# Splitting mixed tiles into f16 parts first and turning them by transposing DMAs

## The chip, the cores and the metric

The kernel runs on one core of a Trainium2 chip. The metric is the device time of one execution in microseconds, the median of the runs; a profiled execution gives the trace. Engines: PE multiplies matrices (PEld loads its weights), DVE, ACT and POOL work elementwise, SP issues most DMAs.

## The reference

One layer of a bidirectional encoder over 4096 tokens and 16 prepended meta tokens, width 1024. Two head groups stand side by side; their outputs are joined, gated and projected:

```python
u = rmsnorm(h, norm_g[i])
proj = jnp.einsum('bld,de->ble', u, w_in[i])
f_in, f_gate, q, k, v, a_gate = jnp.split(proj, SPLIT_POINTS, axis=-1)
f_out = fourier_branch(f_in, w_fmix[i], b_fmix[i]) * jax.nn.silu(f_gate)
a_out = attention_branch(q, k, v, q_norm_g[i], k_norm_g[i], cos, sin, n_tok) * jax.nn.silu(a_gate)
mixed = jnp.concatenate([f_out, a_out], axis=-1)
h = h + jnp.einsum('ble,ed->bld', mixed, w_out[i])
```

`fourier_branch` is the real part of a 2-D DFT over positions and 64 channels in 8 groups, then a linear map per group. `attention_branch` has 8 query heads and 2 key/value heads of 64, over all 4112 tokens. A final RMSNorm follows.

## The kernel before

Products of f32 precision are made from f16 parts: a number x is kept as its f16 rounding and the f16 remainder ("hi" and "lo"), and three f16 matmuls (hi by hi, hi by lo, lo by hi) stand for one f32 matmul.

`phase_a` projects all tokens and prepares the Fourier inputs. `phase_b`, which the change touches, has these stages.

- An early loop. The Fourier half is made in units (`seq`: 8 even, one odd remainder, 8 odd, one last): `dft_units` multiplies by DFT matrices into `pd`, `gather` copies `pd` to the f32 tile `stk` on ACT (L870 to L873), `trans` turns `stk` on PE (L895) and splits it to `thl` on ACT, DVE and POOL (L897 to L902), and `mix` applies the linear map on PE (L86 to L88), adds the bias and multiplies by the gate `fgu`. In this loop `mix` evicts PSUM with two ACT instructions (L949) and POOL adds the bias (L954) and multiplies (L956). The result `mo`, f32, is stored to `mf_d` in DRAM by the next `release`. Seven units pass here, while PE also computes row maxima of scores (L1040, reduced on DVE at L1041).
- 32 pairs: 8 blocks of 512 queries by 4 head pairs. `stream` gives a pair 66 steps (two heads by 33 key tiles). Step j makes a score tile on PE (`qk`, L1108 and L1109, into one of two PSUM buffers `s`), its exponential on ACT (L1112), and the f16 remainder on POOL or DVE (L1114). The weighted sum with the values (`pvm`, L1129 to L1136) runs LAG = 5 steps behind. Pairs 0 to 3 also carry the other ten Fourier `mix` units, through `block0`; there DVE evicts and adds the bias (L951) and POOL multiplies (L956).
- In pairs 4 to 31 the output projection of the block before goes along, 128 tokens for each pair. At step TR = 12 `out_tr` takes the f32 Fourier tile `mf` (128x512, loaded from `mf_d`) and the f32 attention tile `obs` (128x512), turns both by eight PE transposes into a PSUM tile of the `m` buffers (L1172), makes the hi part on ACT (L1175), and one step later the lo part on DVE (`low`, L1177). `out_units` then makes 24 matmuls for each of two column halves, one for each step from O0 = 15 and O1 = 39 on (L1189); its index j counts three matmuls for each of eight row blocks, four of `mf` first, then four of `obs`.
- A tail for the last block: `tail_tr(s, part)` transposes `mf` or `obs` of row tile s (L1354) and splits it into `hv` and `lv`, which lie in the buffers of `qA` and `qB`; `tail_mm` and `tail_end` project and normalise.

The order of instructions on each engine is the order in which the code emits them; an engine does not pass a waiting instruction. The DMAs named here go through SP's queue in program order.

## Time and profile before

| | |
|---|---|
| median of three runs | 3243.61 us (3240.65 to 3244.94) |
| span of the profiled execution | 3240.9 us |
| TensorE clock granted, mean | 0.997 |
| from the transposes of pair 4 to those of pair 31 (L1172 starts at 1140.1 and ends its starts at 3128.9) | 27 pairs, 73.7 us each |

The profiled execution's own time is not listed apart from the three runs; its span lies 2.7 us under their median. In rows of instructions the first two numbers are start and length in us, then engine, line, operation, output tile<-inputs and shape; what stands in square brackets is the time that the engine was idle before, and what ended it. In groups, "x28: a/b/c" gives count and least, median and greatest length in ns.

### The profile page before, as it was taken

Reading aid. Unit: us, or ns where it says so; the run is one execution under the profiler, and the core shown is the slowest. Engines: PE = TensorE matmul, PEld = TensorE weight load, DVE = VectorE, ACT = ScalarE, POOL = GpSimd, SP = SyncE. Lnnn points to the kernel's source line nnn. Section 1 sums busy time; section 2 is a strip of 40 time slices with the busy share of each in tenths; the row PEclk is TensorE's granted clock in tenths of the full one; section 3 lists DMA queues with packets and bytes.
Section 4 is the critical chain, followed back from the end, with each engine's and each line's share of the span. In section 5 each row is a group of like instructions: output and inputs, shape, how many; then the busy total and the mean of one; then the engine's idle time right before and its main releaser. Section 6 shows DMA issues by size and latency. Waiting matters only on the chain.

```text
span 3240.9 us, 78233 instructions
## 1 busy us (share of the span) xinstructions
PE 3189.1 (98%) x32919; PEld 1879.4 (58%) x32919; DVE 2375.5 (73%) x3246; ACT 1703.2 (53%) x2969; POOL 2264.4 (70%) x2172
## 2 busy tenths in 40 slices
PE   8999999998999999999999999999999999999998
PEld 4665555555666655555555555555555555555564
DVE  7656566647677777777777778777777877778764
ACT  5443433434555555555555555555555555555553
POOL 4655455536777778777777777777787777777762
PEclk9999999999999999999999999999999999999999
DMA  7443344638322210002001000100110020000011
GB/s 249 134 160 138 136 154 145 198 140 250 118 78 85 77 50 21 21 21 63 21 21 47 21 21 24 47 21 21 33 52 21 21 47 21 25 21 21 21 37 59
DMA packets 139572, 232.00 MB, mean 72 GB/s; under 512 B 22131, under 2 KB 78275, under 8 KB 136275
## 3 DMA queue, kind: packets, MB, share of 16 engines
q1 hardware_dynamic: 125394, 201.83, 19.8%
q10 hardware_dynamic: 13824, 25.17, 2.1%
q8 instruction: 257, 4.21, 0.5%
q14 instruction: 97, 0.79, 0.1%
HBM read 160.58 MB, written 66.38 MB: 70 GB/s over the span
## 4 chain that ended last, share of the span: by engine, by line
PE 91%; DVE 4%; issue 2%; DMA 1%; ACT 1%; POOL 1%; SPq 0%; ACTq 0%; POOLq 0%; DVEq 0%
PE s L1109 14%; PE s L1108 14%; PE o L1129 13%; PE po L1189 9%; PE m L1040 8%; PE o L1136 8%; PE ps L303 5%; PE ps L304 5%; PE ps L306 4%; PE o L1134 2%; PE o L1132 2%; PE pd L857 2%; PE m L1369 1%; PE m L1172 1%; PE pf L86 1%
## 5 line engine op out<-in xcount | busy, mean ns | idle before, releaser
L1114 POOL TENSOR_TENSOR rr<-pe 128x512 f16<-128x512 f32 x1572 | 1680.3, 1085 | 523.4 <-ACT pe L1112 517.9
L1112 ACT ACTIVATE pe<-s 128x512 f32<-128x512 f32 x2112 | 1260.3, 597 | 1031.8 <-PE s L1109 880.6
L1041 DVE TENSOR_REDUCE mx<-m 128x2 f32<-128x1024 f32 x1024 | 1205.7, 1219 | 174.7 <-PE m L1040 169.3
L1136 PE MATMUL o<-VV,rr 128*128 128x65 f16 x8448 | 975.9, 193 | 0.0
L1136 PEld LDWEIGHTS <-rr 128*128 128x128 f16 x8448 | 785.5, 98 | 168.8 <-POOL rr L1114 1.5
L1129 PE MATMUL o<-VV,pe 128*128 128x129 f16 x6336 | 841.0, 222 | 0.5 <-ACT tt L1140 0.4
L1109 PE MATMUL s<-qB,K 128*128 128x512 f16 x2112 | 800.6, 379 | 1.4 <-DVE qB L1076 1.4
L1129 PEld LDWEIGHTS <-pe 128*128 128x128 bf16 x6336 | 591.2, 98 | 362.1 <-issue 191.3
L1108 PE MATMUL s<-qA,K 128*128 128x512 f16 x2112 | 799.8, 379 | 0.7 <-ACT pe L1112 0.7
L1114 DVE TENSOR_TENSOR rr<-pe 128x512 f16<-128x512 f32 x540 | 450.5, 835 | 230.3 <-ACT pe L1112 225.9
L1132 PE MATMUL o<-VV,pe 128*128 128x65 f16 x2112 | 411.5, 195 | 0.0
L1134 PE MATMUL o<-VV,pe 128*128 128x64 f16 x2112 | 410.7, 194 | 0.0
L303 PE MATMUL ps<-wh,xh 128*128 128x512 f16 (+2 forms) x1032 | 353.3, 354 | 8.0 <-ACT xh L291 8.0
L304 PE MATMUL ps<-wl,xh 128*128 128x512 f16 (+2 forms) x1032 | 353.1, 354 | 2.7 <-DVE wl L274 2.7
L1040 PE MATMUL m<-K,qP 64*128 64x512 f16 x2048 | 313.2, 382 | 6.5 <-DMA qP<-q_d 2.4
L306 PE MATMUL ps<-wh,xl 128*128 128x512 f16 x768 | 292.1, 380 | 0.0
L1134 PEld LDWEIGHTS <-pe 128*128 128x128 bf16 x2112 | 209.2, 99 | 0.0
L1132 PEld LDWEIGHTS <-pe 128*128 128x128 bf16 x2112 | 206.6, 98 | 0.0
L1109 PEld LDWEIGHTS <-K 128*128 128x128 f16 x2112 | 205.2, 97 | 1.7 <-issue 1.6
L1108 PEld LDWEIGHTS <-K 128*128 128x128 f16 x2112 | 203.5, 96 | 0.9 <-issue 0.4
L1040 PEld LDWEIGHTS <-qP 64*128 64x128 f16 x2048 | 59.9, 94 | 226.5 <-issue 224.0
L1189 PE MATMUL po<-woh,mh 128*128 128x512 f16 x448 | 169.8, 379 | 0.9 <-DVE hh L1194 0.9
(213 smaller groups left out, 3561.1 us busy)
## 6 DMA issues: line engine op xcount, KB each, us to landing
room<-x SPq DMA_DIRECT2D x32, 512.0 KB
xt<-xt SPq DMA_DIRECT2D x32, 512.0 KB
sg<-fx SPq DMA_DIRECT2D x16, 1024.0 KB
xr<-x SPq DMA_DIRECT2D x32, 512.0 KB
out<-yo SPq DMA_DIRECT2D x32, 512.0 KB
ct<-cdo SPq DMA_DIRECT2D x9, 1088.0 KB
fg_d<-g ACTq DMA_DIRECT2D x32, 256.0 KB
ag_d<-g ACTq DMA_DIRECT2D x32, 256.0 KB
```

What stands on the lines that cost most here:

```text
L303: T.matmul(o, xh[:, d, :n], wh[:, d, c0:c1], start=d == 0, stop=False)
L304: T.matmul(o, xh[:, d, :n], wl[:, d, c0:c1], start=False, stop=False)
L1040: T.matmul(t[:, e], q[rs, s, p], K[kv][rs, 4 * c:4 * c + 4, 0], start=True, stop=True)
L1041: V.tensor_reduce(mx[:, s, :, c], t, axis=AX.X, op=ALU.max)
L1108: T.matmul(s, K[kv][:, t, 0], qa, start=True, stop=False)
L1109: T.matmul(s, K[kv][:, t, 1], qb, start=False, stop=True)
L1112: S.activation(pe, s, AF.Exp, scale=HD ** -0.5)
L1114: eng.tensor_tensor(out=rr, in0=pe, in1=hi, op=ALU.subtract)
L1129: T.matmul(o[:, c0:c0 + 129], hi[:, cs], va, start=t == 0 and s == 0, stop=t == NT, skip_group_check=True)
L1132: T.matmul(o[:, c0:c0 + 65], hi[:, cs], vh, start=False, stop=t == NT, skip_group_check=True)
L1134: T.matmul(o[:, c0:c0 + 64], hi[:, cs], vl, start=False, stop=t == NT, skip_group_check=True)
L1136: T.matmul(o[:, c0:c0 + 65], rr[:, cs], vh, start=False, stop=t == NT, skip_group_check=True)
```

## The change

The mixed tiles are split into hi and lo parts before they are turned, and the turning is done by DMAs that transpose 2-byte data.

- Fourier half: `mix` itself makes the two f16 parts, hi on ACT and lo on POOL, for both halves (`ver`) of a unit, and `mf_d` holds 1024 f16 numbers for a token in place of 512 f32 (the same bytes). The parts lie in `hlx` or in the buffers of `mt` and `at`.
- Attention half: `out_tr` makes hi from `obs` on ACT, `low` makes lo on DVE and issues the transposing DMA into `at`.
- `load_mf` is now a transposing DMA from `mf_d` into `mt`, issued at step 53 of the pair ahead.
- The matmuls read `mt` and `at`; the 224 PE transposes of pairs 4 to 31 are gone.
- Tail: eight transposing DMAs at step 20 of the last pair bring the Fourier halves into `hv` and `lv`; `tail_tr` turns the attention half alone, with 16 PE transposes in place of 32.

```diff
+        bs = w2.tile([P, 2, 512], F32, tag="xr", name="bs")
+        bias, stk8 = bs[:, 0], bs[:, 1]
+        hlx = w2.tile([P, 2, 2, 512], F16, tag="xr", name="hlx")
+        hls = [[hlx[:, i] for i in range(2)],
+               [w1.tile([P, 2, 512], F16, tag=n, name="hl" + n) for n in ("mt", "at")]]
...
             G.tensor_tensor(out=mo[:n], in0=mo[:n], in1=fgs.pop(u)[:n], op=ALU.mult)
+            hl = hls[u % 2]
             for ver in range(2):
+                S.activation(hl[ver][:n, 0], mo[:n, ver], AF.Copy)
+                G.tensor_tensor(out=hl[ver][:n, 1], in0=mo[:n, ver], in1=hl[ver][:n, 0], op=ALU.subtract)
                 for p0, m, t0, st in runs_of(u, ver):
-                    held.append((rows(mf_d, t0, m, st), mo[p0:p0 + m, ver]))
+                    held.append((rows(mf_d, t0, m, st), hl[ver][p0:p0 + m].rearrange("p w c->p (w c)")))
...
         def load_mf(b, s):
-            mf = w2.tile([P, 512], F32, tag="mf", name="mf")
-            dma(mf, mf_d[b * QB + s * P:b * QB + s * P + P])
-            pst[b, s] = [mf, None]
+            mt = w1.tile([P, 8, P], F16, tag="mt", name="mt")
+            dma_t(mt, mf_d[b * QB + s * P:b * QB + s * P + P])
+            mts[b, s] = [mt]
...
         def out_tr(b, s):
-            mf, xr = pst[b, s]
-            t = pm.tile([P, 2, 512], F32, tag="m", name="m")
-            tv = t.rearrange("p a (b c)->p (a b) c", c=P)
-            for j in range(8):
-                src = mf[:, j * P:(j + 1) * P] if j < 4 else obs[b][:, s, (j - 4) * P:(j - 3) * P]
-                T.transpose(tv[:, j], src, id32)
-            mh = ld["sh1"].tile([P, 8, P], F16, tag="mh", name="mh")
-            ml = ld["sh1"].tile([P, 8, P], F16, tag="ml", name="ml")
-            S.activation(mh, tv, AF.Copy)
-            pst[b, s] = [mh, ml, xr]
-            return lambda: V.tensor_tensor(out=ml, in0=tv, in1=mh, op=ALU.subtract)
+            src = obs[b][:, s]
+            hl = ld["sh1"].tile([P, 2, 512], F16, tag="ml" if s % 2 else "mh", name="ah")
+            S.activation(hl[:, 0], src, AF.Copy)
+
+            def low():
+                V.tensor_tensor(out=hl[:, 1], in0=src, in1=hl[:, 0], op=ALU.subtract)
+                at = w1.tile([P, 8, P], F16, tag="at", name="at")
+                dma_t(at, hl.rearrange("p w c->p (w c)"))
+                mts[b, s].append(at)
+
+            return low
...
-                T.matmul(d["po"], (ml if w == 2 else mh)[:, i],
+                T.matmul(d["po"], mts[b, s][i // 4][:, i % 4 + (4 if w == 2 else 0)],
...
             if i > 4:
-                out_load(b - 1, p)
+                load_xr(b - 1, p)
...
+                if i >= 4 and j == 53 and i + 1 < len(pairs):
+                    load_mf(*divmod(i - 3, 4))
...
                 if j == 20 and i + 1 == len(pairs):
-                    load_mf(b, 0)
-                    load_mf(b, 1)
+                    for x in range(4):
+                        t0 = b * QB + x * P
+                        dma_t(hv[:, 8 * x:8 * x + 4], mf_d[t0:t0 + P, 0:512])
+                        dma_t(lv[:, 8 * x:8 * x + 4], mf_d[t0:t0 + P, 512:1024])
                     load_xr(b, 0)
...
-        def tail_tr(s, part):
-            src = pst[b, s][0] if part == 0 else obs[b][:, s]
+        def tail_tr(s):
+            src = obs[b][:, s]
```

The changed code is longer, so line numbers move: L949 is L953 in the changed kernel, L956 L960, L1112 L1119; the copies in `mix` are L963, its subtractions L964, `load_mf` L1162, `low`'s DMA L1177.

Three places in the order of instructions. The first is ACT in the early loop, from one unit's eviction to the next, before and now (`mo` the mixed unit, `stk` the gathered next one, `thl` its split):

```order
L949 ACTIVATE mo<-s 128x512 x2
L870 ACTIVATE stk<-pd 128x4x64
L872 ACTIVATE stk<-pd 128x4x2
L873 ACTIVATE stk<-pd 128x4x2x31
L897 ACTIVATE thl<-s 128x512
L898 ACTIVATE thl<-thl 128x512
L949 ACTIVATE mo<-s 128x512 x2
```

```order
L953 ACTIVATE mo<-s 128x512 x2
L963 ACTIVATE hlx<-mo 128x512 x2
L874 ACTIVATE stk<-pd 128x4x64
L876 ACTIVATE stk<-pd 128x4x2
L877 ACTIVATE stk<-pd 128x4x2x31
L901 ACTIVATE thl<-s 128x512
L902 ACTIVATE thl<-thl 128x512
L953 ACTIVATE mo<-s 128x512 x2
```

Two copies, which read `mo` after POOL's multiplication, now stand ahead of the next unit's gather. The second place is ACT in pairs 0 and 1, around the first odd unit (`pe` the exponentials, `tt` a head's eviction):

```order
L897 ACTIVATE thl<-m 128x512
L898 ACTIVATE thl<-thl 128x512
L1112 ACTIVATE pe<-s 128x512 x13
L1140 ACTIVATE tt<-o 128x452
L1112 ACTIVATE pe<-s 128x512 x5
```

```order
L901 ACTIVATE thl<-m 128x512
L902 ACTIVATE thl<-thl 128x512
L1119 ACTIVATE pe<-s 128x512 x11
L963 ACTIVATE hlmt<-mo 128x512
L963 ACTIVATE hlat<-mo 128x512
L1119 ACTIVATE pe<-s 128x512 x2
L1147 ACTIVATE tt<-o 128x452
L1119 ACTIVATE pe<-s 128x512 x5
```

The two copies of the unit stand between two exponentials. The third place is SP in two consecutive pairs of the steady part:

```order
L1222 DMA out<-yo 128x1024
L1155 DMA mf<-mf_d 128x512
L1160 DMA xr<-x 128x1024
L811 DMA ag<-ag_d 128x4x128
L1222 DMA out<-yo 128x1024
```

```order
L1224 DMA out<-yo 128x1024
L1162 DMA_TRANSPOSE mt<-mf_d 128x8x128
L1167 DMA xr<-x 128x1024
L811 DMA ag<-ag_d 128x4x128
L1177 DMA_TRANSPOSE at<-ah 128x8x128
L1224 DMA out<-yo 128x1024
```

The load of the Fourier half is a transposing DMA, and a second one, for the attention half, stands between the gate load and the store of the output.

## Prediction

> **What bounds the kernel now.** I read the page's busy times and the chain that ended last first, then the sums over four stretches of the span, and only then single instructions where the diff puts new ones. On the page:

> ```profile
> span 3240.9 us, 78233 instructions
> PE 3189.1 (98%) x32919; PEld 1879.4 (58%) x32919; DVE 2375.5 (73%) x3246; ACT 1703.2 (53%) x2969; POOL 2264.4 (70%) x2172
> PE 91%; DVE 4%; issue 2%; DMA 1%; ACT 1%; POOL 1%; SPq 0%; ACTq 0%; POOLq 0%; DVEq 0%
> ```

> PE carries nine tenths of the chain, so PE time taken away should come off the end, and PE time lost to a new wait should be added to it. By stretch (start:end, length, busy time of PE, PEld, DVE, ACT, POOL, granted clock, DMA):

> ```profile
> 720.00:797.00 77.00, 63.40 (x577) 41.94 (x575) 54.93 (x66) 29.87 (x63) 48.20 (x30) 1.00 0.72 224
> 797.00:1116.00 319.00, 313.80 (x3809) 206.72 (x3808) 229.69 (x238) 170.56 (x312) 245.82 (x240) 1.00 0.33 101
> 1140.00:3100.00 1960.00, 1959.84 (x22709) 1132.43 (x22708) 1549.68 (x1787) 1116.01 (x1887) 1524.53 (x1544) 1.00 0.10 30
> ```

> The first is the early Fourier loop (PE 82%), the second the attention pairs 0 to 3 with Fourier units mixed in (98%), the third attention with the output projection (100%). The removed transposes lie in the third and in the tail; the new splits of the Fourier half lie in the first two, which the words of the change do not tell.

> **Steady part: transposes removed.** PE in the last pair, at the step with the transposes, and one ACT group:

> ```profile
> 3128.53 0.60 PE L1172 MATMUL m<-id,mf 128*128 128x128 f32 x4
> 3128.97 0.60 PE L1172 MATMUL m<-id,ob 128*128 128x128 f32 x4
> 3129.40 0.22 PE L1129 MATMUL o<-VV,pe 128*128 128x129 f16 x1
> L1175 ACT ACTIVATE mh<-m x28: 1023/1023/1024, 1141.2 to 3129.6; 128x1024 f16<-128x1024 f32 x28
> ```

> Eight transposes take 3129.40 - 3128.53 = 0.87 us of PE's queue, 28 times: -24.4 us. Since PE has no idle time there, all of it should come off. The split that stays becomes half as long on ACT and DVE and reads SBUF; both have slack (57% and 79% of the third stretch), so I cost it at nothing.

> What must now be in time is the transposing DMA into `at`: issued at step 13, first read at step 27. The thirteenth projection matmul of the last pair, and the one long DMA that the chain shows:

> ```profile
> 3143.82 0.38 PE L1189 MATMUL po<-woh,mh 128*128 128x512 f16 x1
> 820.42 12.79 DMA acs<-acs_d
> ```

> That step is the tightest: no maximum units lie between. Without the transposes the matmul comes at 3142.95; I put the f16 parts ready near 3130.4 (step 13 at 3128.9, and 1.5 us for copy and subtraction), which leaves 12.5 us. `acs<-acs_d` moves 2 MB in 12.79 us, so 256 KB at that rate are 1.6 us; the upper bound I take is that whole 12.79, which would just cost nothing or a few tenths. So: cost 0, ends 0 and some 10 us. `mt` is issued at step 53 and read at step 15 of the next pair, twice as long. On SP's queue `at` stands behind the gate load, the queue's longest waiter:

> ```profile
> SPq L811 <- POOL ob L1146: 1157.0, 30, 68.4
> ```

> It waits for POOL's output rows of the previous pair's second head, which by the lag of five steps come at step 4 or 5, so the queue is free before step 13; behind `at` stands only the output store. The eight DMAs of the last pair have from step 20 to the pair's end, over 40 us.

> **Tail.**

> ```profile
> 3203.10 0.60 PE L1354 MATMUL s<-id,mf 128*128 128x128 f32 x4
> 3210.03 0.66 PE L1354 MATMUL s<-id,mf 128*128 128x128 f32 x4 [0.71 <-DVE qB L1358]
> ```

> Sixteen transposes go (16 x 0.109 = 1.7 us), and the 0.71 us wait for a PSUM buffer that the `mf` transposes of row tile 2 filled: -2.5 us.

> **Early loop: the new wait.** mix() now puts two ACT copies behind ACT's two evictions. They read what POOL's multiplication writes, and ACT's next work (gather and split of the following unit) stands behind them. One unit before, from add to add on POOL, with the ACT, PE and DVE rows of the next unit:

> ```profile
> 746.43 2.34 POOL L954 TENSOR_TENSOR mo<-mo,bias 128x1024 f32<-128x1024 f32 x1 [4.67 <-DMA bias<-bias]
> 782.74 2.36 POOL L954 TENSOR_TENSOR mo<-mo,bias 128x1024 f32<-128x1024 f32 x1 [1.50 <-ACT mo L949]
> 785.18 2.35 POOL L956 TENSOR_TENSOR mo<-mo,fgu 128x1024 f32<-128x1024 f32 x1
> 789.59 2.35 POOL L954 TENSOR_TENSOR mo<-mo,bias 128x1024 f32<-128x1024 f32 x1 [1.50 <-ACT mo L949]
> 783.35 0.38 ACT L870 ACTIVATE stk<-pd 128x256 f32<-128x256 f32 x1 [0.68 <-PE pd L854]
> 783.68 0.39 ACT L873 ACTIVATE stk<-pd 128x248 f32<-128x248 f32 x1
> 784.12 0.66 PE L895 MATMUL s<-id,stk 128*128 128x128 f32 x4
> 786.51 0.68 DVE L901 TENSOR_TENSOR thl<-s,thl 128x512 f16<-128x512 f32 x1
> L378 ACT ACTIVATE qs<-t 128x512 f16<-128x512 f32 x32 | 19.9, 623 | 46.4 <-POOL t L363 46.4
> L1114 POOL TENSOR_TENSOR rr<-pe 128x512 f16<-128x512 f32 x1572 | 1680.3, 1085 | 523.4 <-ACT pe L1112 517.9
> ```

> Before, ACT gathers the next unit while POOL works, and the cycle is POOL's add, multiplication, copy and 1.50 us of waiting: 6.85 us. After, it is a ring through four engines: add to end of multiplication 4.79 (782.74 to 787.53), signal 0.08 (as from the add's end, 785.10, to 785.18), two copies 2 x 0.623 = 1.25 (L378 is the same shape), gather 0.72 with 0.05 on either side, transposes to DVE's subtraction 2.39 (784.12 to 786.51), from there to the next add 3.08 (786.51 to 789.59): 12.4 us. POOL's two subtractions, about 1.09 each as L1114, end inside it. Six cycles stand from 746.43 to 789.59, 43.2 us; six of 12.4 are 74.4: +31.3. Behind the seventh unit the first attention step waits likewise:

> ```profile
> 790.30 0.39 ACT L873 ACTIVATE stk<-pd 128x248 f32<-128x248 f32 x1
> 796.29 0.38 PE L1109 MATMUL s<-qB,K 128*128 128x512 f16 x1 [1.41 <-DVE qB L1076]
> ```

> The gather ends 1.10 after the add before (790.69) and 6.94 after it then, 5.8 later; I take 4.9, since the DVE work on the row maxima ahead of qB goes on meanwhile. Early loop: +36.2 us, between 28 (gather partly covered) and 42.

> **Pairs 0 to 3: the same wait in front of the exponentials.** Ten more units end there. ACT's copies stand behind one exponential and ahead of the next; PE has two score buffers, so it stops at the third score matmul on. The multiplication, the exponential that would follow, and that third score matmul, for the first unit, and multiplication and matmul for the last:

> ```profile
> 805.83 2.36 POOL L956 TENSOR_TENSOR mo<-mo,fgu 128x1024 f32<-128x1024 f32 x1 [1.82 <-DVE mo L951]
> 805.07 0.60 ACT L1112 ACTIVATE pe<-s 128x512 f32<-128x512 f32 x1 [1.92 <-PE s L1109]
> 807.15 0.38 PE L1108 MATMUL s<-qA,K 128*128 128x512 f16 x1
> 1112.39 2.34 POOL L956 TENSOR_TENSOR mo<-mo,fgu 64x1024 f32<-64x1024 f32 x1 [1.83 <-DVE mo L951]
> 1113.84 0.38 PE L1108 MATMUL s<-qA,K 128*128 128x512 f16 x1
> ```

> Copies and exponential end 0.08 + 1.25 + 0.03 + 0.60 + 0.04 = 2.0 us after the multiplication. First unit: 808.19 + 2.0 - 807.15 = 3.0 us of PE standing; last: 1114.73 + 2.0 - 1113.84 = 2.9; the eight between come to 2.4 to 3.4 by the same rows, the ten to 28.7. PE has 2% of idle there to give back, so: +28.7 us, between 22 and 34. The weighted sums run five steps behind, so POOL's subtractions (2 x 1.09) delay nothing there.

> **The clock.** Idle stretches of PE and what the clock did:

> ```profile
> 323.54 0.27 PE L221 MATMUL pr<-id,rall 128*5 128x128 f32 x1 [3.51 <-DVE ko L391]
> 323.54:327.45 3.91, 3.91 (x11) 1.51 (x12) 3.56 (x5) 1.03 (x3) 1.02 (x1) 0.56 0.33 95
> 830.84:833.25 2.41, 0.00 (x1) 0.00 (x0) 1.84 (x3) 0.60 (x1) 1.03 (x1) 1.00 0.22 84
> 833.25:837.00 3.75, 3.75 (x44) 2.36 (x44) 1.09 (x1) 1.19 (x2) 1.72 (x2) 1.00 0.45 140
> ```

> After 3.51 us idle PE got 0.56 of its clock for 3.91 us and lost about 1.7 us of work; after 2.41 nothing. In the ring PE idles over 5 us per unit, always enough: some 1.0 us of its share of the ring each, 7 in all. The stops of 2.4 to 3.4 lie between the two rows: I count four of ten at 1.7, 7 us, with ends 0 and 17. [...]

> **Sum.** -24.4 - 2.5 + 36.2 + 28.7 + 7 + 7 = +52 us. The profiled span of 3240.9 becomes 3293; the median of the runs is 3243.6, 2.7 more, so I forecast 3296.

> **Rivals.** (a) Faster, 3217: ACT's wait is absorbed, and only -24.4 - 2.5 counts. It would need the ring and the stops to cost under 27 us together, 1.6 us for each of 17 units, where the rows give 5.2 and 2.9; for it speaks only that ACT is 53% busy. 6%. (b) Half: the stops in the pairs are caught up by the lag of five steps, the ring is not: 3243.6 - 27 + 36 + 7 = 3260. Against it speaks that PE, in order, cannot pass a score matmul that has no buffer. 8%. (c) The transposes land late, at 18 us where pairs with maximum units leave about 15: 27 x 3 + 5 = 86 more, 3382. Nothing in the trace shows a transposing DMA. [...] 10%. (d) The forecast, 76%, 3270 to 3322 by the ends of its terms. The range takes in (b) and leaves (a), (c) and the forecast's edges out. What a measurement of this kernel tells from no change is about 0.2%, 6.5 us: faster holds (a), 6%; the same a weak (b), 4%; slower the rest.

> **What would show it.** Right: ACT's copies at L963 wait for POOL L960 some 5 us each in the early loop and 2 to 4 in the pairs; adds on POOL 12 to 13 us apart; score matmuls after each mix 2 to 3 us late; pairs 4 to 30 0.87 us shorter each; `at` landed before step 27. Wrong: PE waiting for a DMA at the projection's thirteenth matmul, or adds still 7 us apart.

## Result and the profile after

The changed kernel takes 3290.06 us (median of 4 runs, 3288.52 to 3296.02) against 3242.99 us (3240.65 to 3244.94) before: ratio 1.0151, 95% interval 1.0136 to 1.0166, 47 us slower. The forecast was 3296. The page of the profiled execution, its first line, busy times and the chain that ended last:

```profile
span 3287.4 us, 77879 instructions
PE 3178.9 (97%) x32679; PEld 1857.6 (57%) x32679; DVE 2368.9 (72%) x3242; ACT 1703.5 (52%) x2999; POOL 2327.0 (71%) x2206
PE 87%; POOL 4%; DVE 3%; issue 2%; ACT 2%; DMA 2%; SPq 0%; ACTq 0%; POOLq 0%; DVEq 0%
```

PE does 10 us less work (3189.1 to 3178.9) in a span 46.5 us longer. POOL's share of the chain rose from 1% to 4%: PE now waits for others. Where it waits is read from three score matmuls on PE, the first of all, the first of pair 4 and the last of this line, before (L1108) and after (L1115):

```profile
794.51 0.38 PE L1108 MATMUL s<-qA,K 128*128 128x512 f16 x1
1127.35 0.61 PE L1108 MATMUL s<-qA,K 128*128 128x512 f16 x1
3182.34 0.38 PE L1108 MATMUL s<-qA,K 128*128 128x512 f16 x1
```

```profile
841.16 0.38 PE L1115 MATMUL s<-qA,K 128*128 128x512 f16 x1
1199.59 0.38 PE L1115 MATMUL s<-qA,K 128*128 128x512 f16 x1
3231.81 0.38 PE L1115 MATMUL s<-qA,K 128*128 128x512 f16 x1
```

Up to the first score matmul +46.7 us; pairs 0 to 3 358.4 against 332.8, +25.6; pairs 4 to 31 2032.2 against 2055.0, -22.8; from there to the end (3287.4 - 3231.81 against 3240.9 - 3182.34) -3.0. Together +46.5, the difference of the spans.

**The early loop.** One ring after the change, POOL's add to POOL's add, in order of time:

```profile
788.66 2.34 POOL L958 TENSOR_TENSOR mo<-mo,bs 128x1024 f32<-128x1024 f32 x1 [1.60 <-ACT mo L953]
793.46 0.63 ACT L963 ACTIVATE hlmt<-mo 128x512 f16<-128x512 f32 x1 [4.87 <-POOL mo L960]
795.26 1.12 PE L899 MATMUL s<-id,stk 128*128 128x128 f32 x4 [3.82 <-ACT stk L877]
799.11 1.23 DVE L1048 TENSOR_REDUCE mx<-m 128x2 f32<-128x1024 f32 x1 [6.07 <-PE m L1047]
800.25 0.68 DVE L905 TENSOR_TENSOR thl<-s,thl 128x512 f16<-128x512 f32 x1
803.17 2.34 POOL L958 TENSOR_TENSOR mo<-mo,bs 128x1024 f32<-128x1024 f32 x1 [1.50 <-ACT mo L953]
```

ACT's copy of the upper part waits 4.87 us for POOL's multiplication; behind it in ACT's queue stands the gather, for which PE's transposes of the next unit wait 3.82 us, and so on round to POOL. This ring takes 14.5 us, the longest of six. The seven adds run from 747.60 to 829.80 (746.43 to 789.59 before): 13.7 us a cycle in place of 7.2, +39.0 for six. The last add to the first score matmul takes 11.36 us in place of 4.92, +6.4, and the execution came to the loop 1.2 us later: 46.7. The transposes took 1.12 us in place of 0.66 and the granted clock of this stretch fell:

```profile
720.00:840.00 120.00, 74.16 (x569) 46.68 (x568) 54.83 (x67) 35.36 (x75) 63.53 (x43) 0.79 0.47 146
842.00:1199.00 357.00, 326.21 (x3914) 213.45 (x3914) 239.81 (x246) 183.41 (x338) 274.09 (x266) 0.99 0.29 89
1200.00:3130.00 1930.00, 1929.83 (x22414) 1102.80 (x22414) 1538.31 (x1779) 1098.27 (x1882) 1543.49 (x1538) 1.00 0.12 33
```

(Columns as in the prediction: length, busy PE, PEld, DVE, ACT, POOL, then the clock.) In the 120 us of the first row PE is busy 74, at 0.79 of its clock: after a first stretch of 10.24 us at half clock come six of 6.83 us, 13.65 us from start to start, about one for each ring.

**Pairs 0 to 3.** What PE waited for there, the two largest rows after and before:

```profile
PE s L1115 <- ACT pe L1119: 22.3, 11, 2.9
PE o L1136 <- ACT tt L1147: 3.0, 1, 3.0
```

```profile
PE m L1071 <- DVE nm L1064: 3.8, 2, 3.1
PE pd L857 <- DMA acs<-acs_d: 2.4, 1, 2.4
```

All of PE's waits in this stretch add up to 31.1 us after and 9.6 before, +21.5. The rest is PE's busy time, 327.2 us in place of 323.2: after the change three stretches of 3.41 us run at half clock, each behind one of the stops. The kernel before has one too, 6.83 us long behind a wait of 3.07 us for `nm`; 4.6 us of it lie ahead of pair 4's first score matmul, the other 2.2 in pair 4.

**Steady pairs.** PE is busy 1929.83 of 1930.00 us, and no transposing DMA is waited for. One `at`, the issue on SP's queue and what the DMA engines moved over 2525 to 2535 us, in slices of 0.25 us:

```profile
2525.81 1.23 SPq L1177 DMA_TRANSPOSE at<-ah  x1
GB/s 0 33 0 0 0 0 0 5 194 218 212 206 189 26 0 66 0 0 0 0 0 0 0 0 0 0 0 0 0 0 0 0 0 0 0 0 0 0 0 0
```

1.2 us of issue and 1.3 us of traffic at some 200 GB/s, over by 2528.5, 2.7 us from the start of the issue (the 66 that follows is one 16 KB packet of another queue). Its first reader, fourteen steps on, comes 14.8 us after that start; over the 28 transposes it is 13.8 to 14.8 us, and 11.2 in the last pair.

### The profile page after: what moved, and what is told of

It reads as the page before. It is cut to its first block, busy times and chain, and to the rows that moved or that the text cites. A ratio compares the mean times of both kernels' runs of the same rounds, so it can differ in the third digit from the quotient of the medians.

```text
span 3287.4 us, 77879 instructions
## 1 busy us (share of the span) xinstructions
PE 3178.9 (97%) x32679; PEld 1857.6 (57%) x32679; DVE 2368.9 (72%) x3242; ACT 1703.5 (52%) x2999; POOL 2327.0 (71%) x2206
## 4 chain that ended last, share of the span: by engine, by line
PE 87%; POOL 4%; DVE 3%; issue 2%; ACT 2%; DMA 2%; SPq 0%; ACTq 0%; POOLq 0%; DVEq 0%
PE s L1115 13%; PE s L1116 13%; PE o L1136 12%; PE po L1191 9%; PE m L1047 8%; PE o L1143 8%; PE ps L303 5%; PE ps L304 5%; PE ps L306 4%; PE o L1141 2%; PE o L1139 2%; PE pd L861 2%; POOL rr L1121 1%; PE m L1374 1%; POOL mo L960 1%
## 5 line engine op out<-in xcount | busy, mean ns | idle before, releaser
L1121 POOL TENSOR_TENSOR rr<-pe 128x512 f16<-128x512 f32 x1572 | 1704.8, 1102 | 472.1 <-ACT pe L1119 465.8
L1119 ACT ACTIVATE pe<-s 128x512 f32<-128x512 f32 x2112 | 1258.8, 597 | 999.9 <-PE s L1116 861.3
L1115 PE MATMUL s<-qA,K 128*128 128x512 f16 x2112 | 800.2, 379 | 22.6 <-ACT pe L1119 22.6
L1121 DVE TENSOR_TENSOR rr<-pe 128x512 f16<-128x512 f32 x540 | 458.0, 849 | 239.7 <-ACT pe L1119 218.3
L1116 PEld LDWEIGHTS <-K 128*128 128x128 f16 x2112 | 205.2, 97 | 24.4 <-issue 24.3
L1115 PEld LDWEIGHTS <-K 128*128 128x128 f16 x2112 | 203.5, 96 | 0.9 <-issue 0.4
L1191 PE MATMUL po<-woh,mt 128*128 128x512 f16 x448 | 169.8, 379 | 1.0 <-DVE hh L1196 1.0
```

The costliest lines, as they stand in the source:

```text
L1115: T.matmul(s, K[kv][:, t, 0], qa, start=True, stop=False)
L1116: T.matmul(s, K[kv][:, t, 1], qb, start=False, stop=True)
L1119: S.activation(pe, s, AF.Exp, scale=HD ** -0.5)
L1121: eng.tensor_tensor(out=rr, in0=pe, in1=hi, op=ALU.subtract)
```

## Experiments

### Both splits later, one place at a time

In these kernels mix() puts its split on a list, from which it is emitted later: in the early loop by trans(), two units on (the first lines below), in pairs 0 to 3 by block0(), in steps 5, 6 and 7 behind the mix (the last line). The core of the edit, with gaps marked by dots:

```diff
+                if early and len(splits) > 1:
+                    f = splits.pop(0)[1]
+                    f[0]()
+                    f[1]()
+                    f[2]()
+                    behind.append(f[3])
...
-                S.activation(hl[ver][:n, 0], mo[:n, ver], AF.Copy)
-                G.tensor_tensor(out=hl[ver][:n, 1], in0=mo[:n, ver], in1=hl[ver][:n, 0], op=ALU.subtract)
+            splits.append((now[0] + 5, [lambda: hi(0), lambda: hi(1), lambda: lo(0, G), lambda: lo(1, V)]))
...
+            if splits and g >= splits[0][0]:
...
```

> The change as it is, but each Fourier unit's split (two ACT copies, two subtractions) is emitted later: in the early loop two units later, behind that unit's ACT copies of the transposed sums, with two more buffers for the unit's result; in pairs 0 to 3 five, six and seven steps after the mix, one ACT copy to a step. One subtraction of each unit goes to DVE, the other stays on POOL. Theory A (the loss is ACT standing in order behind POOL's multiplication): the first score matmul comes back from 841.2 us to 794.5 to 801, pairs 0 to 3 come back from 358.4 us to 333 to 339, and the 22.8 + 3.0 us won in the steady pairs and the tail stay: 3243 - 26 + 0 to 12 = 3217 to 3229 us, I take 3221. Theory B (the loss is the added work itself, 18 units of two copies of 0.62 and two subtractions of 1.16 us on engines that have no room in these stretches): at most the waits change name, and the time stays above 3270 us.

> Only the early loop's splits are emitted later (as in the kernel with both); in pairs 0 to 3 they stand where the change put them. Theory A: the 46.7 us before the first score matmul come back but for 0 to 6, pairs 0 to 3 stay 25.6 us longer than before the change: 3290 - 47 + 0 to 6 = 3243 to 3249 us. Theory B: 3285 us or more. If the two places interact, the gain here and that of the kernel with only the pairs' splits moved do not add up to that of both, by more than 5 us.

> Only the splits in pairs 0 to 3 are emitted later; in the early loop they stand where the change put them. Theory A: the stops of PE at the third score matmul behind a mix go (22.6 us of waiting for ACT's exponential down to under 3) and with them the three half-clock stretches: 3290 - 26 + 0 to 6 = 3264 to 3270 us. Theory B (the lag of five steps would have caught the stops up, the 25.6 us are POOL's and ACT's added work): 3285 us or more.

Both: 3236.89 us (3233.94 to 3239.27), ratio 0.9982 (0.9973 to 0.9991). Early loop alone: 3262.14, 1.0065 (1.0052 to 1.0078). Pairs alone: 3268.63, 1.0083 (1.0069 to 1.0097). Against 3290 the early loop's splits give back 28 us, the pairs' 21, both 53: the places add up within the 5 us allowed. (In the first two the parts of a unit are overwritten before their store is issued: in the kernel with both, those of unit 5 go into `hlmt` at 801.70 us, those of unit 7 at 822.01, and the store of unit 5 is issued at 830.94, counting units from 0. Those rows come out wrong; the operations and their sizes are the same.)

The pairs' case is as theory A says: PE's waits for ACT's exponential there go from 22.3 to 0.5 us, and the stretch comes to 3.8 us above before.

```profile
PE s L1127 <- ACT pe L1131: 0.5, 2, 0.3
```

In the early loop the direction is right but theory A's size was missed, 8 to 13 us too slow: of the 46.7 us before the first score matmul 8.7 stay with both moved (12.3 with the early loop alone), and pair 0 is 8.2 us longer; with the early loop alone pair 0 is 11.9 us longer than in the changed kernel. The rows of the kernel with both, on DVE, POOL and PE, show two causes that the expectation had left out:

```profile
771.24 2.35 POOL L967 TENSOR_TENSOR mo<-mo,bs 128x1024 f32<-128x1024 f32 x1 [0.39 <-ACT mo L962]
772.14 2.00 DVE L976 TENSOR_TENSOR hlat<-moe,hlat 128x512 f16<-128x512 f32 x1
773.67 2.67 POOL L969 TENSOR_TENSOR mo<-mo,fgu 128x1024 f32<-128x1024 f32 x1
PE pd L862 <- DMA acs<-acs_d: 6.2, 1, 6.2
```

The subtraction I gave to DVE takes 2.00 us where POOL's takes 1.16, and POOL's multiplication beside it 2.67 in place of 2.35; and six held stores (the expectation for the kernel with both on POOL says five; before the change there are two) stood ahead of the Fourier operand's load on SP's queue, for which PE waited 6.2 us in place of 2.4. The kernel with both splits on POOL, below, takes the two away together, so what each cost is not shown apart.

### The split alone

The kernel before the change, with TensorE transposes and f32 Fourier rows, and only this added:

```diff
+                S.activation(hl[:n, ver, 0], mo[:n, ver], AF.Copy)
+                G.tensor_tensor(out=hl[:n, ver, 1], in0=mo[:n, ver], in1=hl[:n, ver, 0], op=ALU.subtract)
```

> The kernel before the change, with its TensorE transposes and its f32 tensor for the Fourier half, and only the split added where the change puts it: its f16 parts go to two otherwise idle buffers that nothing reads. Theory A: it costs what the change loses in the early loop and pairs 0 to 3, 46.7 + 25.6 = 72 us, and wins nothing: 3243 + 72 = 3315 us, 3308 to 3322. Rival C (part of the loss comes from the transposing DMAs, the f16 stores or the moved loads): 3300 us or less.

3318.70 us (3317.59 to 3319.53), ratio 1.0236 (1.0222 to 1.025): theory A, rival C falls. ACT's and PE's waits in it (from 720 to 1200 us, and from 800 to 1180):

```profile
ACT hl L960 <- POOL mo L957: 83.3, 17, 8.0
PE s L1112 <- ACT pe L1116: 19.9, 10, 2.9
PE pd L858 <- ACT stk L874: 6.3, 1, 6.3
```

By stretch it is +46.3, +29.3, -0.7 and 0.0: the losses of the change without its gains. No transposing DMA, f16 store or moved load has a part in them.

### Both splits later, on POOL

The edit against the first kernel with both splits later (left out: held stores also go out ahead of each split, and in the early loop the second subtraction is emitted with the first):

```diff
-                splits.append((now[0] + 5, [lambda: hi(0), lambda: hi(1), lambda: lo(0, G), lambda: lo(1, V)]))
+                splits.append((now[0] + 5, [lambda: hi(0), lambda: hi(1), lambda: lo(0, G), lambda: lo(1, G)]))
...
-                    release()
                     if arg == 8:
                         ld["acs_load"](1)
+                    release()
```

> Both places' splits emitted later, as in the first kernel of that kind, with three differences: all subtractions are on POOL (there DVE's took 1.6 to 2.0 us beside POOL's work, in a queue that holds up TensorE's maximum units), the load of the second Fourier operand is issued ahead of the held stores (five stores stood in front of it and PE waited 6.2 us for it, 2.4 before the change), and held stores are released ahead of each split. Theory A, as it stands now (the wait is gone, what is left is the added work where a queue has no room): POOL's cycle in the early loop is 2.35 + 2.35 + 0.61 + 2 x 1.16 = 7.6 to 7.9 us against 6.85, so the first score matmul comes 5 to 7 us later than before the change, pairs 0 to 3 take 2 to 7 us more, and 24.5 come off behind: 3242 - 24.5 + 7 to 14 = 3224 to 3232 us, I take 3229. Theory B' (what is left comes from the added work whichever queue does it): 3236 us again.

3219.95 us (3219.38 to 3222.71), ratio 0.9937 (0.9924 to 0.9949), and measured a second time 3219.37 (3216.90 to 3223.02), 0.993 (0.9917 to 0.9944). It beats the kernel before by 0.6 to 0.7% and the changed one by 70 us. Theory A holds, B' falls. The time is 4 us below A's range: the first score matmul comes 2.5 us later than before where 5 to 7 were given, and pairs 0 to 3 take 0.6 us more where 2 to 7 were given. PE, the first score matmul and the first of pair 4, and POOL in the early loop:

```profile
797.05 0.38 PE L1130 MATMUL s<-qA,K 128*128 128x512 f16 x1
1130.48 0.61 PE L1130 MATMUL s<-qA,K 128*128 128x512 f16 x1
767.82 1.16 POOL L976 TENSOR_TENSOR hlmt<-moe,hlmt 128x512 f16<-128x512 f32 x1
768.94 1.16 POOL L976 TENSOR_TENSOR hlat<-moe,hlat 128x512 f16<-128x512 f32 x1
770.05 2.35 POOL L967 TENSOR_TENSOR mo<-mo,bs 128x1024 f32<-128x1024 f32 x1
```

The add follows the subtraction with no wait: POOL is now the early loop's bound, at 7.5 us a cycle where nothing else disturbs it (four of six). By stretch +2.5, +0.6, -23.1, -3.0.

### The upper part copied by POOL

```diff
-                S.activation(hl[ver][:n, 0], mo[:n, ver], AF.Copy)
+                G.tensor_copy(hl[ver][:n, 0], mo[:n, ver])
```

> The change with the splits where it puts them, but the f16 upper parts are copied by POOL in place of ACT, so no ACT instruction stands behind POOL's multiplication; POOL gets two copies a unit more (0.6 to 1.1 us each). Theory A (it is ACT's wait): the stops at the third score matmul go, the early cycle is POOL's own chain, add, multiplication, two copies, two subtractions, copy and 1.5 us of waiting, 10.3 to 11.3 us: +21 to 27 in the early loop, 0 to 8 in pairs 0 to 3, and -25.5 behind: 3242 - 25.5 + 21 to 35 = 3238 to 3252 us, I take 3245. Theory B (it is the work, of which POOL now has more): 3285 us or more.

3263.25 us (3260.63 to 3264.12), ratio 1.0068 (1.0054 to 1.0082): between the theories. The early loop is as A says (+24.3), and the stops for ACT's exponential are gone; but pairs 0 to 3 cost 20.7 where I gave at most 8, by a new wait:

```profile
PE o L1143 <- POOL rr L1121: 17.2, 13, 2.2
```

Multiplication, two copies of 0.61 and two subtractions of 1.15 hold POOL for 5.9 us at one go, and its remainders of the weights come later than the lag of five steps covers. So it is no property of ACT: with the split taken whole and at once, POOL's queue handed the delay to what stands behind it just as ACT's did.

### How late may the transposing DMA be

```diff
-                if j == TR + 1 and b > 0:
+                if j == TR + 7 and b > 0:
                     low()
```

In the second kernel it is TR + 13.

> The change, but the lower part and the transposing DMA of the attention half are emitted at step 19 in place of 13; its first reader stays at step 27, 9.9 us later (8 us in the last pair). If the transposing DMA lands 3.2 us after its issue, as the DMA engines' busy time shows, with 0.8 us of subtraction ahead of it: no change, 3290 us, within 4. [...]

> The same at step 25, 2.6 us ahead of the first reader (2.0 in the last pair). With 0.8 us of subtraction and 3.2 us from issue to landing PE stops some 1.5 us in each of 28 pairs: 3290 + 28 x 1.5 = 3332 us, 3315 to 3350. [...] If it lands as soon as its 1.3 us of traffic allow: 3290 us.

Step 19: 3290.82 us (3289.29 to 3292.27), ratio 1.0154 (1.014 to 1.0168), as with step 13. Step 25: 3387.47 us (3383.39 to 3392.16), 1.0457 (1.0441 to 1.0473), 97 us more where 42 were expected. In the second, PE's waits behind pair 3 and the DVE, SP and PE rows of one row tile:

```profile
PE po L1191 <- DMA at<-ah: 72.1, 28, 3.2
1305.28 0.68 DVE L1175 TENSOR_TENSOR ah<-ob,ah 128x512 f16<-128x512 f32 x1
1306.11 1.26 SPq L1177 DMA_TRANSPOSE at<-ah  x1
1309.22 0.39 PE L1191 MATMUL po<-woh,at 128*128 128x512 f16 x1 [2.57 <-DMA at<-ah]
```

From issue to reader it is 3.11 us (3.07 to 3.14 over the 28). The 3.2 of the expectation had taken the packet of the other queue for the end of the transpose; that it came so near is luck. The stop is 2.57 and not 1.5 because the subtraction starts only 1.4 us before PE comes to the reader (1306.65), not 2.6: I had counted from the step at which it is emitted, and DVE is behind PE there. 72.1 us are the stops. Of the other 25 some 14 are the half clock behind nine of them (a pair with such a stretch is 1.6 us longer than the like pair without), and 3.7 lie in pairs 0 to 3; the rest is not broken down.

### One remainder moved to DVE

In the kernel with both splits late on POOL, in pairs 5 to 31:

```diff
+            if i > 4:
+                on_dve.add(8)
```

> The kernel with both places' splits late (3220 us), and in pairs 5 to 31 the rounding remainder of the weights of step 8 is taken by DVE in place of POOL. Theory A (without the transposes' 0.87 us PE reaches step 14 before POOL has the remainder it reads there, 0.13 us lost in three pairs of four): POOL's chain of five remainders ends 1.1 us earlier, the waits of PE's weight loads for POOL's remainder (some 0.3 us, 22 in the changed kernel) go, pairs become 0.87 us shorter than before the change in place of 0.73: 20 x 0.13 = 2.6 us less, 3217 us. Rival (the 0.13 us come from elsewhere, or DVE's maxima come late instead): steps 14 and 15 stay or others grow, 3220 us or more.

> The kernel with both places' splits late once more, on the same chip as the one above, as its comparison: 3220 us, 3217 to 3223.

3228.49 us (3227.19 to 3229.21), ratio 0.9958 (0.9945 to 0.997), 9 us slower than the kernel without the move (3219.37): the rival. Step 14 went from 0.92 to 0.79 us as expected, but step 11 from 0.79 to 1.19. The weight loads' waits without and with the move, then, in the same order, the busy time of both engines with remainders in 3.6 us round that step (length, DVE, POOL):

```profile
PEld L1158 <- POOL rr L1136: 6.0, 21, 0.3
```

```profile
PEld L1158 <- POOL rr L1136: 14.2, 25, 0.6
```

```profile
2304.90:2308.50 3.60, 1.01 (x1) 3.11 (x3) 1.00 0.28 77
```

```profile
2309.80:2313.40 3.60, 2.45 (x2) 3.08 (x3) 1.00 0.27 77
```

DVE's two remainders take 2.45 us where one that runs with POOL idle takes 0.68, and the one of POOL's beside the second of them 1.48 instead of 1.03, so that it ends 0.45 us later and PE stands at step 11; DVE's next maximum starts 1.1 us later too.

## Why the prediction was right

Point by point, by its own steps:

- **Transposes removed, -24.4:** measured -22.8 for pairs 4 to 31, and some 0.7 of that has another source: pair 4 is 1.53 us shorter, because before the change its first 2.2 us ran at half clock. The kernel with the split alone keeps the transposes and is 0.7 us shorter there too. The term was oversized by the part that PE gives back: without its 0.87 us at step 12 it reaches step 14 before POOL has the remainder it needs there, and most pairs are 0.73 to 0.75 us shorter, only each fourth the whole 0.87. The prediction named no next waiter here; to ask what is late next would have found POOL's five remainders in a row. The weight loads' waits for them, before and after:

```profile
PEld L1136 <- POOL rr L1114: 0.4, 1, 0.4
PEld L1143 <- POOL rr L1121: 6.3, 22, 0.4
```

  That the wait sits in POOL's chain is shown by step 14 (0.92 to 0.79) in the last experiment.
- **Split and transposing DMA in the steady part, 0:** right. 1.3 us of traffic where 1.6 were worked out from the `acs` load's rate, and 3.1 us from issue to reader where PE does wait for it (step 25). The 18 us of rival (c) are shown by no run; it fell on the 3290.82 of step 19.
- **Tail, -2.5:** -3.0.
- **Early loop, +36.2 and +7 for the clock:** 39.0 + 6.4 = 45.4 against 43.2 (the other 1.2 us lie ahead of the loop). The ring was the right mechanism, 13.7 us a cycle against 12.4 + 1.0. The part undersized is from the transposes to DVE's subtraction: 5.0 us (795.26 to 800.25 in the ring shown) where 2.39 and 1.0 for the clock stood, since at half clock the maximum unit ahead of it in DVE's queue came late too (DVE waited 6.07 us for PE there); from the end of the eviction to the gather's end the ring was 0.3 us shorter than taken, behind the subtraction 0.2.
- **Pairs 0 to 3, +28.7 and +7:** 25.6. The ten stops are 1.9 to 3.0 us long, 24.9 together in place of 28.7; PE's older waits (3.8 for DVE's `nm` among them) went in under them, -3.4; and PE's busy time, where the clock shows, grew by 4.0 in place of 7, since three stops of ten halved the clock, not four, and the half-clock stretch of the kernel before went with its wait. How many halve it differs between executions: in the two kernels with the transposing DMA later, the same code here, the half clock lasts five windows of 3.41 us in place of three, and the stretch is 29.2 us longer than before.
- **The signs named:** ACT's copies wait 4.87 us in the early loop (some 5 were given), but 4.4 to 5.1 in the pairs where 2 to 4 were given; the adds are 13.0 to 14.5 us apart, not 12 to 13. `at` landed in time.
- **Rivals (a) and (b):** both fell; the waits were not absorbed. What (a) would need is what the best kernel does: 3220 against its 3217, reached by moving the split away from the multiplication, not by slack.

The sum, +52.0 forecast and +46.5 measured, is off by what the pairs were oversized (-10.1), less what the early loop and the steady pairs came out worse (+3.4 and +1.6), and -0.5 in the tail. The mechanism was right in the early loop and in pairs 0 to 3, where the loss lies; that the total came within 6 us is in part luck, since the errors go both ways.

## What to carry to other kernels

Before a copy is put in an in-order queue, ask what it reads and who finishes that last; two copies of 0.62 us cost 2 to 6.5 us a unit because they stood directly behind a 2.35 us producer on another engine, and the same copies two units or five steps later, with both subtractions on POOL, cost 2.5 and 0.6 us in all. Work taken off the bound engine paid here in the stage where that engine had no idle time, and in most pairs only up to the next engine's chain (0.73 to 0.75 of 0.87 us), while the ten stops put into another stage, 24.9 us together, made that one 25.6 us longer. When moving leftover work between VectorE and GpSimd, price it with the other engine running, not by a row where it ran alone: a remainder of 0.68 us on DVE with POOL idle took 1.00 and 1.52 us beside POOL's work in the last experiment.

## What was not expected of the hardware

```profile
1307.03:1310.45 3.42, 1.23 (x14) 1.00 0.40 77
1310.45:1313.86 3.41, 3.41 (x24) 0.50 0.00 0
1382.13:1385.54 3.41, 1.65 (x16) 1.00 0.36 69
1385.54:1388.95 3.41, 2.62 (x35) 1.00 0.04 8
```

Behind the window with 64% idle the clock was 0.50, behind the one with 52% it stayed 1.00. Laid on the grid, the nine stops that halved fill 64 to 75% of a window and the nineteen others at most 59%. So stops of nearly one length cost a half-clock window or nothing by where they fell on the grid. The idle share gives no sharp threshold either: in the changed kernel, on its own grid, the window from 963.46 us is 57% idle and the next ran at 0.50, the one from 854.23 is 59% idle and the next ran at 1.00. A stop of 2.57 us was enough for a half-clock window at 1310.45. The prediction's bracket, between 2.41 us that did nothing and 3.51 that halved the clock, is therefore no threshold in length, and the kernel before had a row between, which the prediction passed over:

```profile
1123.58 0.29 PE L1071 MATMUL m<-id,nm 128*128 128x128 f16 x1 [3.07 <-DVE nm L1064]
1123.58:1129.59 6.01, 6.01 (x42) 3.23 (x43) 2.53 (x3) 1.79 (x3) 1.46 (x2) 0.50 0.00 0
```

Behind 3.07 us of idling PE ran 6.01 us at half clock.

**Where VectorE and GpSimd subtracted SBUF tiles at once, nearly every subtraction ended by the other engine's instruction:** 0.54 to 0.66 us behind it on DVE, 0.90 us behind it on POOL. DVE and POOL round step 11 of the last experiment, in order of time:

```profile
2309.75 0.61 POOL L1169 TENSOR_TENSOR ob<-ob,rc 128x256 f32<-128x256 f32 x1
2309.90 1.00 DVE L1136 TENSOR_TENSOR rr<-pe 128x512 f16<-128x512 f32 x1
2310.32 1.49 POOL L1136 TENSOR_TENSOR rr<-pe 128x512 f16<-128x512 f32 x1
2310.83 1.52 DVE L1136 TENSOR_TENSOR rr<-pe 128x512 f16<-128x512 f32 x1
2311.77 1.48 POOL L1136 TENSOR_TENSOR rr<-pe 128x512 f16<-128x512 f32 x1
```

They end at 2310.36, 2310.90, 2311.81, 2312.35 and 2313.25: each DVE subtraction some 0.55 us behind the POOL operation that ran when it started, each POOL subtraction 0.90 us behind DVE's. So it is through the whole trace of the changed kernel. Of the 568 subtractions of two SBUF tiles in DVE's remainders and lower parts, 56 start with POOL idle and take 0.67 to 0.69 us; 512 start while a POOL operation runs, and 509 of them end 0.54 to 0.66 us after it. Of POOL's 1572 remainders 242 start during such a DVE subtraction, and 238 of them end 0.90 us after it; nearly all others take 1.04. DVE's maxima, which read PSUM, take 1.15 to 1.23 us with POOL busy or idle. In the first kernel with both splits late it is the same: DVE's subtraction ends at 774.14, 0.55 us behind POOL's add (773.59), and the multiplication that starts meanwhile is 0.32 us longer. That the two engines wait for each other there is read from these times; why they do is shown by no run here.
